# Down projection of an encoder layer: low parts of weights on VectorE alone, and quarter sums in another form

## The chip, the cores and the metric

The kernel runs on one core of a Trainium2 chip. The metric is the device time of one execution in microseconds (us), the median over several runs. Five engines work beside each other, each through its own queue in order: TensorE (PE; PEld is its weight load), VectorE (DVE), ScalarE (ACT), GpSimd (POOL), and SyncE (SP), which here only issues transfers. Engines wait for each other by semaphores.

## The reference

One encoder layer in float32 on a sequence of 1024 positions with 1024 features. The change is in its last large product:

```
x = x + g1 * (concat(y_attn, y_mem) @ w_out)
h = modulate(rms_norm(x, norm_ffn_g), sh2, sc2)
ffn = (silu(h @ w_gate) * (h @ w_up)) @ w_down      # (1024 x 2816) @ (2816 x 1024)
x = x + g2 * ffn
return rms_norm(x, final_norm_g)
```

## The kernel before

**Numbers.** Every float32 matrix is split into a high part (rounded to fp32r by a ScalarE copy, `hi`) and a low part (the rest, `lo`, a subtraction `src - hi`). A product is three matmuls: high x high, low x high and high x low (`mm3`, lines 298 to 300). In the tile names of the profile `wch` and `wcl` are the high and low part of a weight piece of the down projection, `whi` and `wlo` those of a piece of the activations; `wst` is the staging tile into which the activations come from DRAM.

**Seven products instead of eight.** The down projection is cut into 2 x 2 blocks and done by Winograd's form of Strassen's scheme, in the order of `DOWN`: 11, 21, T2, T3, T1, 22, T4. Each product runs over 11 pieces of the hidden dimension, and a piece is 4 row tiles x 3 matmuls of 128x128 by 128x512 (T4 runs twice at half width). The first five pieces of product 11 are made earlier by other code. For piece p the weights are in two tiles `wd` of 128x1024: `WD[0,p]` holds the quarters a11 and a21, `WD[1,p]` holds a12 and a22. In the rows below `wd_11122` to `wd_11126` and `wd_11105` to `wd_11110` are `WD[0,0]` to `WD[0,10]`, and `wd_11111` to `wd_11121` are `WD[1,0]` to `WD[1,10]`; `s` is a tile of 128x512 for a sum. The weights of the products are 11: a11; 21: a12; T2: a21 + a22 - a11; T3: a11 - a21; T1: a21 + a22; 22: a12 - (a21 + a22 - a11); T4: a22. Quarters that are not needed any more are overwritten by sums, in place.

**What makes a weight piece.** `load_w` (line 1487) takes the next (product, piece), and chains: the flags that must be set (`ok`), the sums (`steps`, on VectorE), `hi` on ScalarE, `lo`. The low part is made on VectorE for the products 11, 21, 22 and T4, and on GpSimd for T2, T3 and T1 (`eng`). `wch` and `wcl` have four buffers each, so a piece's high part waits until TensorE is through with the piece four before. GpSimd also makes the low parts of the activations, one per piece (`split`, line 436). At the end of a product VectorE adds the four banks in PSUM to the rows of x, once for each cell that the product belongs to (`finish`, line 1558: 16 additions for 11, 4 for 21, 12 for T2, 8 for T3, 8 for T1). After product 21 four rows are complete; ScalarE squares them (`ssb`, `sqb`) and VectorE sums the squares (`ssb<-ssb,sqb`).

**The order.** The program is recorded by a planner (`Clock`) that keeps an estimated time for each engine; `ck.chain` records each step when the planner's clock reaches it, so an edit of the steps moves the order of instructions on the engines around it. On the chip each engine follows that order, and the semaphores only delay it.

Of the kernel before, what the change touches and what calls it, by code (L numbers as in the profile page):

```python
# [11 lines left out]
F32 = mybir.dt.float32  # L12
# [8 lines left out]
P = 128  # L21
# [3 lines left out]
HALF = 512  # L25
# [215 lines left out]
def layer_kernel(ctx, tc, xT, c, w_ada, vecs, cons, rope, w_f, w_t0, w_t, w_o, w_gu, w_d, out):  # L241
# [65 lines left out]
    def halves(n):  # L307
        return slice(n * HALF, (n + 1) * HALF)

    ck = Clock()  # L310
    dve, act, gps = Engine(ck, nc.vector, "dve"), Engine(ck, nc.scalar, "act"), Engine(ck, nc.gpsimd, "gps")
# [39 lines left out]
    with tc.manual_schedule():  # L351
# [1103 lines left out]
        WE = {q: [None, None, Flag()] for q in wseq}  # L1455
        todo = []

        def open_down():
            rest = []

            def rows(c, p):
                WD[c, p] = pb.tile([P, D], F32, tag=f"wd{c}{p}", name=f"wd{c}{p}")
                rest.append((lambda: WD[c, p], w_d[2 * p + c], wd_ok[c, p]))

            for p in range(KB, NP):
                rows(0, p)
            for p in range(NP):
                rows(1, p)
            for p in range(KB):
                rows(0, p)  # L1470
            todo[0:0] = rest[0:NP - KB]
            reload("T4")
            todo.extend(rest[NP - KB:])
            opened3.set(ck, ck.t)
            load_rows()
            for _ in range(4):
                load_w()
# [9 lines left out]
        def load_w():  # L1487
            if not wseq:
                return
            q = m, c, p = wseq.pop(0)  # L1490
            e = WE[q]
            if m == "T4":
                if c == 0:
                    t = pb.tile([P, 2, HALF], F32R, tag=f"wd0{p}", name="a22")
                    e[:2] = t[:, 0], t[:, 1]
                    WE[m, 1, p] = e
                    a22 = WD[1, p][:, halves(1)]
                    ck.chain(0.0, lambda: act.activation(t[:, 0], a22, AF.Copy),
                             lambda: dve.tensor_sub(t[:, 1], a22, t[:, 0].bitcast(F32)), flag=e[2])
                return  # L1500
            a11, a12, a21, a22 = (WD[x, p][:, halves(r)] for r in range(2) for x in range(2))
            src = {"11": a11, "21": a12, "T3": a11, "T1": a21, "22": a12, "T4": a22}.get(m)
            ok = [wd_ok[x, p] for x in ((0,) if m in ("11", "T3") else (1,) if m in ("21", "22", "T4") else (0, 1))]
            steps = []
            if m == "T2":
                src = pb.tile([P, HALF], F32, tag="s", name="s", bufs=3)
                steps = [lambda: dve.tensor_add(src, a21, a22), lambda: dve.tensor_sub(src, src, a11),
                         lambda: dve.tensor_sub(a12, a12, src)]
            elif m == "T3":
                steps = [lambda: dve.tensor_sub(a11, a11, a21)]  # L1510
            elif m == "T1":
                steps = [lambda: dve.tensor_add(a21, a21, a22)]
            eng = dve if m in ("11", "21", "22", "T4") else gps

            def hi():
                e[0] = pb.tile([P, HALF], F32R, tag="wch", name="wch", bufs=4)
                act.activation(e[0], src, AF.Copy)

            def lo():
                e[1] = pb.tile([P, HALF], F32R, tag="wcl", name="wcl", bufs=4)  # L1520
                eng.tensor_sub(e[1], src, e[0].bitcast(F32))

            ck.chain(0.0, *ok, *steps, hi, lo, flag=e[2])

        def down():
            i = start["down"]
            flat = lambda t: t.rearrange("p a b -> p (a b)")
            for m in DOWN:
                for c in range(2 if m == "T4" else 1):
                    w = 256 if m == "T4" else HALF  # L1530
                    banks = []
                    for p in range(NP):
                        t = pieces[i]
                        early = m == "11" and p < KB
                        a = pieces[i + 1] if early else WE[m, c, p]
                        i += 2 if early else 1
                        yield [t[2], a[2]]
                        wt = [flat(x) for x in a[:2]] if early else a[:2]
                        for o in range(4):
                            if p == 0:  # L1540
                                yield [slot("acc")]
                                banks.append(psum_tile([P, w], "acc"))
                            mm3(banks[o][0], [x[:, o * P:(o + 1) * P] for x in wt], [flat(x) for x in t[:2]],
                                p == 0, p == NP - 1)
                            ck.pe(0.65 * w / HALF)
                        load_piece()
                        if early:
                            load_piece()
                        if opened3.done and not early:
                            load_w()  # L1550
                        if m == "22" and p < 4:
                            load_w()
                        load_rows()
                    finish(m, c, banks)
# [427 lines left out]
        pb = ctx.enter_context(tc.tile_pool(name="pb", bufs=1))  # L1982
# [80 lines left out]
```

## Time and profile before

| what | value |
|---|---|
| median of 3 runs | 1428.02 us (1427.50 to 1428.83) |
| the profiled execution | 1430.91 us, span 1429.1 us |
| mean granted TensorE clock | 0.967 |
| busy in the span: PE, DVE, ACT, POOL | 1312.8 us (92%), 1078.9 us (75%), 660.8 us (46%), 792.5 us (55%) |
| first matmul of 21, T2, T3, T1, 22, T4 | 1209.17, 1240.00, 1285.53, 1319.81, 1351.71, 1382.07 us |

Times in the rows of the trace are in us from the start of the span: start, duration, engine, line, operation, tile written, tiles read. A bracket at the end of a row tells how long the engine had been idle before it and what ended that. Nearly all of VectorE, ScalarE and GpSimd has line 96, the helper that records an instruction, so rows are told apart by tiles.

### The profile page before, as it was taken

Reading aid. Unit: us, or ns where it says so; the run is one execution under the profiler, and the core shown is the slowest. Engines: PE = TensorE matmul, PEld = TensorE weight load, DVE = VectorE, ACT = ScalarE, POOL = GpSimd, SP = SyncE. Lnnn points to the kernel's source line nnn. Section 1 sums busy time; section 2 is a strip of 40 time slices with the busy share of each in tenths; the row PEclk is TensorE's granted clock in tenths of the full one; section 3 lists DMA queues with packets and bytes.
Section 4 is the critical chain, followed back from the end, with each engine's and each line's share of the span. In section 5 each row is a group of like instructions: output and inputs, shape, how many; then the busy total and the mean of one; then the engine's idle time right before and its main releaser. Section 6 shows DMA issues by size and latency. Waiting matters only on the chain.

```text
span 1429.1 us, 19533 instructions
## 1 busy us (share of the span) xinstructions
PE 1312.8 (92%) x6602; PEld 1079.3 (76%) x6602; DVE 1078.9 (75%) x1542; ACT 660.8 (46%) x1192; POOL 792.5 (55%) x624
## 2 busy tenths in 40 slices
PE   5789799999999989999986999999999999979997
PEld 2578677888877978877764788888888887757786
DVE  6947979986887948677699786676666653999676
ACT  5444326677666655454564333333233234434462
POOL 4555554544345336677658554454454445789942
PEclk8899999999999999999999999999999999989999
DMA  7546452322121155743542333323233259622324
GB/s 280 165 123 198 136 169 78 118 65 64 52 60 58 36 162 181 255 159 122 184 155 72 105 126 103 111 97 104 103 111 111 69 188 330 238 69 87 104 63 152
DMA packets 103172, 184.40 MB, mean 129 GB/s; under 512 B 11296, under 2 KB 32672, under 8 KB 103072
## 3 DMA queue, kind: packets, MB, share of 16 engines
q1 hardware_dynamic: 89968, 161.06, 35.3%
q10 hardware_dynamic: 13104, 22.10, 4.2%
q8 instruction: 52, 0.85, 0.3%
q14 instruction: 48, 0.39, 0.1%
HBM read 136.19 MB, written 43.25 MB: 126 GB/s over the span
## 4 chain that ended last, share of the span: by engine, by line
PE 54%; DVE 21%; issue 8%; DMA 6%; POOL 5%; ACT 4%; SPq 1%; DVEq 0%; ACTq 0%; POOLq 0%
PE acc L299 13%; PE acc L300 13%; PE acc L298 13%; DVE x L96 4%; DVE ada L96 3%; POOL wlo L96 3%; DVE sst L96 3%; PE av L1028 2%; PE T L1009 2%; DVE PT L96 2%; DVE y L96 2%; PE S L977 2%; PE acct L298 2%; PE acct L300 1%; PE acct L299 1%
## 5 line engine op out<-in xcount | busy, mean ns | idle before, releaser
L96 POOL TENSOR_TENSOR wlo<-wst,whi 128x512 fp32r<-128x512 f32 (+2 forms) x208 | 304.9, 1471 | 212.1 <-ACT whi L96 190.0
L96 ACT ACTIVATE whi<-wst 128x512 fp32r<-128x512 f32 (+2 forms) x219 | 131.5, 605 | 128.2 <-DMA wst<-in_w_f_dram 22.0
L96 POOL TENSOR_SCALAR P<-P,sst 128x1024 f32<-128x1024 f32 x64 | 88.6, 1388 | 143.0 <-DVE sst L96 104.8
L299 PE MATMUL acc<-x,whi 128*128 128x512 f32 x352 | 139.9, 397 | 1.1 <-DVE x L96 1.1
L96 POOL TENSOR_TENSOR wlo<-wr,whi 128x512 fp32r<-128x512 f32 x60 | 82.9, 1382 | 80.9 <-ACT whi L96 80.9
L298 PE MATMUL acc<-hh,whi 128*128 128x512 f32 x224 | 98.0, 437 | 12.4 <-ACT hh L96 10.0
L300 PE MATMUL acc<-whi,wcl 128*128 128x512 f32 x244 | 98.2, 402 | 7.1 <-POOL wcl L96 7.0
L298 PE MATMUL acc<-whi,wch 128*128 128x512 f32 x244 | 97.1, 398 | 7.6 <-ACT wch L96 7.6
L96 ACT ACTIVATE P<-S,sst,colq 128x1024 f32<-128x1024 f32 x64 | 77.2, 1206 | 52.4 <-DVE sst L96 48.0
L299 PE MATMUL acc<-hl,whi 128*128 128x512 f32 x224 | 93.4, 417 | 8.5 <-POOL hl L96 4.8
L299 PE MATMUL acc<-wlo,wch 128*128 128x512 f32 x244 | 97.2, 398 | 0.1
L96 DVE SCALAR_TENSOR_TENSOR ada<-ada,cond 128x512 f32<-128x512 f32 (+1 forms) x79 | 79.0, 1008 | 19.6 <-DMA ada<-in_w_ada_dram 14.1
L300 PE MATMUL acc<-hh,wlo 128*128 128x512 f32 x224 | 92.5, 413 | 0.0
L96 DVE TENSOR_TENSOR sg<-acc,sg 128x512 f32<-128x512 f32 x67 | 45.4, 687 | 60.4 <-PE acc L300 60.0
L96 ACT ACTIVATE PT<-T 128x512 fp32r<-128x512 f32 x128 | 71.4, 596 | 39.8 <-PE T L1009 39.0
L96 DVE TENSOR_TENSOR PT<-T,PT 128x512 fp32r<-128x512 f32 x128 | 82.8, 682 | 7.6 <-ACT PT L96 7.5
L96 ACT ACTIVATE whi<-wr 128x512 fp32r<-128x512 f32 x60 | 37.8, 632 | 109.3 <-PE acc L299 47.3
L298 PE MATMUL acct<-whi,hh 128*128 128x256 f32 (+1 forms) x256 | 79.6, 311 | 2.3 <-DVE avt L96 0.9
L96 POOL TENSOR_TENSOR wlo<-s,whi 128x512 fp32r<-128x512 f32 x44 | 59.4, 1351 | 38.0 <-ACT whi L96 32.1
L299 PEld LDWEIGHTS acc<-x,whi 128*128 128x128 f32 x352 | 66.7, 190 | 16.7 <-DVE x L96 1.6
L1009 PE MATMUL T<-con,P 128*128 128x128 f32 x512 | 71.1, 277 | 8.8 <-DVE PT L96 6.1
L96 DVE TENSOR_REDUCE sst<-S 128x1 f32<-128x1024 f32 x64 | 77.7, 1214 | 1.8 <-PE S L977 1.6
(457 smaller groups left out, 3883.3 us busy)
## 6 DMA issues: line engine op xcount, KB each, us to landing
wr<-in_w_gu_dram SPq DMA_DIRECT2D x66, 256.0 KB, 2.8
ada<-in_w_ada_dram SPq DMA_DIRECT2D x64, 256.0 KB, 3.5
wd<-in_w_d_dram SPq DMA_DIRECT2D x22, 512.0 KB, 7.0
wst<-in_w_gu_dram SPq DMA_DIRECT2D x34, 256.0 KB, 3.1
wst<-act_d SPq DMA_DIRECT2D x33, 256.0 KB, 4.3
ada<-in_w_ada_dram SPq DMA_DIRECT2D x16, 512.0 KB, 5.5
wst<-in_w_o_dram SPq DMA_DIRECT2D x32, 256.0 KB, 3.8
act_d<-sg ACTq DMA_DIRECT2D x31, 256.0 KB, 2.1
```

The source lines that it names most:

```text
L96: return fn(*args, **kw)
L298: nc.tensor.matmul(acc, w[0], x[0], start=first, stop=False)
L299: nc.tensor.matmul(acc, w[0], x[1], start=False, stop=False)
L300: nc.tensor.matmul(acc, w[1], x[0], start=False, stop=last)
L977: nc.tensor.matmul(sp[:, halves(n)], qs[:, j * P:(j + 1) * P], k2[g][m][:, halves(n)], start=m == 0, stop=m == 1)
L1009: nc.tensor.transpose(tp[:, k], Pt[q][:, (4 * b + k) * P:(4 * b + k + 1) * P], ident)
L1028: nc.tensor.matmul(av, va[:, k, h // 4], PT[it][m][:, k], start=(k, m) == (0, 0), stop=(k, m) == (NJ - 1, 1))
```

## The change

All weight pieces get their low part from VectorE. The sums have another form. For T2 the piece first does a11 := a11 - a21 in place, which is the weight of T3, and then s := a22 - a11, which is a21 + a22 - the old a11. So T3 has no sum of its own any more and the first sum of T2 falls away: three sums of T2 and one of T3 become two and one deferred. The third, a12 := a12 - s, for product 22, is recorded after T2's low part (`rest`) instead of ahead of its high part. s has five buffers instead of three. Flags of earlier products are added to `ok`, since a11 is overwritten earlier and T3 and 22 now rely on T2's chain.

```diff
-            steps = []
+            steps, rest = [], []
             if m == "T2":
-                src = pb.tile([P, HALF], F32, tag="s", name="s", bufs=3)
-                steps = [lambda: dve.tensor_add(src, a21, a22), lambda: dve.tensor_sub(src, src, a11),
-                         lambda: dve.tensor_sub(a12, a12, src)]
-            elif m == "T3":
-                steps = [lambda: dve.tensor_sub(a11, a11, a21)]
+
+                src = pb.tile([P, HALF], F32, tag="s", name="s", bufs=5)
+                if ("11", 0, p) in WE:
+                    ok.append(WE["11", 0, p][2])
+                ok.append(WE["21", 0, p][2])
+                steps = [lambda: dve.tensor_sub(a11, a11, a21), lambda: dve.tensor_sub(src, a22, a11)]
+                rest = [lambda: dve.tensor_sub(a12, a12, src)]
+            elif m in ("T3", "22"):
+                ok.append(WE["T2", 0, p][2])
             elif m == "T1":
+                ok.append(WE["T3", 0, p][2])
                 steps = [lambda: dve.tensor_add(a21, a21, a22)]
-            eng = dve if m in ("11", "21", "22", "T4") else gps
+            eng = dve
...
-            ck.chain(0.0, *ok, *steps, hi, lo, flag=e[2])
+            ck.chain(0.0, *ok, *steps, hi, lo, *rest, flag=e[2])
```

**How the order moves.** The order of TensorE and of SyncE is the same in both programs. VectorE at the start of T2, right behind the last low part of product 21, before:

```order
L96 TENSOR_TENSOR s<-wd_11122,wd_11111 128x512
L96 TENSOR_TENSOR s<-s,wd_11122 128x512
L96 TENSOR_TENSOR wd_11111<-wd_11111,s 128x512
L96 TENSOR_TENSOR s<-wd_11123,wd_11112 128x512
L96 TENSOR_TENSOR s<-s,wd_11123 128x512
L96 TENSOR_TENSOR wd_11112<-wd_11112,s 128x512
L96 TENSOR_TENSOR s<-wd_11124,wd_11113 128x512
L96 TENSOR_TENSOR s<-s,wd_11124 128x512
L96 TENSOR_TENSOR wd_11113<-wd_11113,s 128x512
L96 TENSOR_TENSOR s<-wd_11125,wd_11114 128x512
```

and at the same place in the changed program:

```order
L96 TENSOR_TENSOR wd_11122<-wd_11122 128x512
L96 TENSOR_TENSOR s<-wd_11111,wd_11122 128x512
L96 TENSOR_TENSOR wcl<-s,wch 128x512
L96 TENSOR_TENSOR wd_11111<-wd_11111,s 128x512
L96 TENSOR_TENSOR wd_11123<-wd_11123 128x512
L96 TENSOR_TENSOR s<-wd_11112,wd_11123 128x512
L96 TENSOR_TENSOR wcl<-s,wch 128x512
L96 TENSOR_TENSOR wd_11124<-wd_11124 128x512
L96 TENSOR_TENSOR wd_11112<-wd_11112,s 128x512
L96 TENSOR_TENSOR s<-wd_11113,wd_11124 128x512
L96 TENSOR_TENSOR wd_11125<-wd_11125 128x512
L96 TENSOR_TENSOR wcl<-s,wch 128x512
```

Each piece has four rows instead of three, and its low part (`wcl<-s,wch`) stands between the sums. Behind either piece of order the four additions of product 21 follow (`x<-acc,mod,x`). Some rows later in the changed program, VectorE around the fourth and fifth piece (`s` of the fourth is made from `wd_11114` two rows ahead of these):

```order
L96 TENSOR_TENSOR wd_11126<-wd_11126 128x512
L96 TENSOR_TENSOR ssb<-ssb,sqb 128x512 x2
L96 TENSOR_TENSOR wd_11105<-wd_11105 128x512
L96 TENSOR_TENSOR s<-wd_11115,wd_11126 128x512
L96 TENSOR_TENSOR ssb<-ssb,sqb 128x512
L96 TENSOR_TENSOR wcl<-s,wch 128x512
L96 TENSOR_TENSOR s<-wd_11116,wd_11105 128x512
L96 TENSOR_TENSOR wd_11106<-wd_11106 128x512
L96 TENSOR_TENSOR wd_11114<-wd_11114,s 128x512
L96 TENSOR_TENSOR wcl<-s,wch 128x512
```

The low part of the fourth piece stands behind all three sums of squares. GpSimd in T3, before:

```order
L96 TENSOR_TENSOR wcl<-wd_11124,wch 128x512
L96 TENSOR_TENSOR wlo<-wst,whi 128x512
L96 TENSOR_TENSOR wcl<-wd_11125,wch 128x512
L96 TENSOR_TENSOR wlo<-wst,whi 128x512
L96 TENSOR_TENSOR wcl<-wd_11126,wch 128x512
```

and GpSimd in the changed program, from the last pieces of the gate and up projections through the whole down projection:

```order
L96 TENSOR_TENSOR wlo<-wr,whi 128x512 x2
L96 TENSOR_TENSOR wlo<-wst,whi 128x512 x71
L96 TENSOR_TENSOR wlo<-wst,whi 128x256 x11
L96 TENSOR_TENSOR x_10971<-x_10971,ny 128x512
```

Only the low parts of activations are left there.

## The prediction

> **What bounds the kernel now.** I began with the waits of TensorE in the last 250 us, because the change touches only the down projection. Then I cut that projection at its products (a product is 11 pieces of 12 matmuls; its first matmul is found by counting). The columns are busy us (and instructions) of PE, PEld, DVE, ACT and POOL, then clock, DMA share and GB/s; the rows are 21, T2, T3, T1 and 22.
>
> ```profile
> PE acc L298 <- ACT wch L96: 7.6, 3, 6.0
> PE acc L300 <- POOL wcl L96: 7.0, 12, 1.3
> ...
> 1209.17:1240.00 30.83, 30.83 (x134) 24.62 (x133) 29.04 (x32) 14.17 (x23) 19.64 (x13) 1.00 0.84 316
> 1240.00:1285.53 45.53, 35.04 (x133) 25.64 (x132) 45.15 (x37) 17.39 (x32) 38.37 (x24) 0.89 0.26 74
> 1285.53:1319.81 34.28, 31.97 (x134) 24.30 (x133) 31.27 (x28) 14.53 (x25) 34.28 (x24) 1.00 0.30 87
> 1319.81:1351.71 31.90, 31.13 (x133) 24.56 (x132) 18.01 (x16) 12.72 (x23) 31.90 (x24) 1.00 0.31 92
> 1351.71:1382.07 30.36, 30.36 (x134) 24.82 (x132) 21.66 (x30) 16.32 (x31) 14.55 (x12) 1.00 0.27 81
> ```
>
> Product 22 runs with TensorE never idle: 30.36 us is what a product costs when its inputs are there (132 matmuls of 0.23 us). Against that T2 loses 15.2 us, T3 3.9 and T1 1.5, together 20.6 us. That is all this change can win. In T2 DVE is full (45.15 of 45.53), in T3 and T1 POOL is (34.28 of 34.28, 31.90 of 31.90). The DMA share is a third or less, so transfers bound none of the three.
>
> How VectorE and GpSimd hinder each other is read from single rows (start, duration):
>
> ```profile
> 1251.36 0.68 DVE L96 TENSOR_TENSOR wd<-wd,s 128x512 f32<-128x512 f32 x1
> 1251.97 0.68 DVE L96 TENSOR_TENSOR ssb<-ssb,sqb 128x512 f32<-128x512 f32 x1
> 1252.57 0.68 DVE L96 TENSOR_TENSOR s<-s,wd 128x512 f32<-128x512 f32 x1
> ...
> 1255.45 1.75 DVE L96 TENSOR_TENSOR wd<-wd,s 128x512 f32<-128x512 f32 x1
> 1257.13 1.76 DVE L96 TENSOR_TENSOR s<-s,wd 128x512 f32<-128x512 f32 x1
> 1258.81 1.77 DVE L96 TENSOR_TENSOR s<-wd,wd 128x512 f32<-128x512 f32 x1
> ...
> 1272.12 1.67 DVE L96 TENSOR_TENSOR wd<-wd,s 128x512 f32<-128x512 f32 x1
> ...
> 1280.23 1.67 DVE L96 TENSOR_TENSOR wd<-wd,s 128x512 f32<-128x512 f32 x1
> ```
> ```profile
> 1265.10 1.74 POOL L96 TENSOR_TENSOR wcl<-s,wch 128x512 fp32r<-128x512 f32 x1
> 1266.80 1.74 POOL L96 TENSOR_TENSOR wlo<-wst,whi 128x512 fp32r<-128x512 f32 x1
> ...
> 1289.81 1.28 POOL L96 TENSOR_TENSOR wlo<-wst,whi 128x512 fp32r<-128x512 f32 x1
> 1291.06 1.30 POOL L96 TENSOR_TENSOR wcl<-wd,wch 128x512 fp32r<-128x512 f32 x1
> 1292.32 1.29 POOL L96 TENSOR_TENSOR wlo<-wst,whi 128x512 fp32r<-128x512 f32 x1
> ```
> ```profile
> 1245.85 2.71 DVE L96 SCALAR_TENSOR_TENSOR x<-acc,mod,x 128x512 f32<-128x512 f32 x4
> ```
> ```profile
> 1245.34 1.74 POOL L96 TENSOR_TENSOR wlo<-wst,whi 128x512 fp32r<-128x512 f32 x1
> ```
>
> While POOL is idle DVE's sums follow each other every 0.60 us. While DVE works on PSUM, POOL's instructions follow each other every 1.25. When both have sums of two SBUF operands they take turns, one of each per 1.70 us. So a POOL turn takes 1.70 - 0.60 = 1.10 from DVE. The eviction that reads PSUM takes no turn: four last 2.71, 0.67 each, with POOL at work until 1247.1. Check of the two prices: from 1255.45 to the next product's first sum at 1281.83 DVE ran 18 sums and POOL 14 instructions; 18 x 0.60 + 14 x 1.10 = 26.2, measured 26.38.
>
> The Trainium skill (SBUF — State Buffer, "Who interferes with whom") says that a VectorE instruction with two SBUF inputs and a GpSimd instruction that reads SBUF exclude each other for the whole instruction, and the loser fully blocks. By that a pair would take 0.60 + 1.25 = 1.85; the rows say 1.70, so turns are taken, with 0.15 overlapped. By the rule's 1.25 the T2 walk below would be 14 x 0.15 = 2.1 us longer and the result 1420.2; the check above speaks for 1.10.
>
> T2 has one more stall of its own, the longest of all:
>
> ```profile
> 1247.98 0.40 PE L300 MATMUL acc<-whi,wcl 128*128 128x512 f32 x1
> 1254.42 0.79 PE L298 MATMUL acc<-whi,wch 128*128 128x512 f32 x1 [6.04 <-ACT wch L96]
> 1255.01 0.63 PE L299 MATMUL acc<-wlo,wch 128*128 128x512 f32 x1
> 1256.70 0.80 PE L300 MATMUL acc<-whi,wcl 128*128 128x512 f32 x1 [1.06 <-POOL wcl L96]
> ```
> ```profile
> 1251.47 0.63 ACT L96 ACTIVATE sqb<-x 128x512 f32<-128x512 f32 x1 [1.30 <-DVE ssb L96]
> 1252.01 0.71 ACT L96 ACTIVATE x<-x,vec 128x512 f32<-128x512 f32 x1
> ...
> 1253.76 0.61 ACT L96 ACTIVATE wch<-s 128x512 fp32r<-128x512 f32 x1
> ```
>
> After three pieces (1240.0 + 3 x 2.76 = 1248.3) TensorE waits for the high part of the fourth. On ScalarE that stands behind the third square of the finished rows, which waits for a VectorE sum.
>
> **The change, part by part.** Three rows give the volume: POOL's low parts of weights, 11 and 22 of them, and the sum that goes.
>
> ```profile
> L96 POOL TENSOR_TENSOR wcl<-s,wch 128x512 fp32r<-128x512 f32 x11 | 18.9, 1719 | 2.7 <-ACT wch L96 2.7
> L96 POOL TENSOR_TENSOR wcl<-wd,wch 128x512 fp32r<-128x512 f32 x22 | 33.7, 1535 | 0.0
> L96 DVE TENSOR_TENSOR s<-s,wd 128x512 f32<-128x512 f32 x11 | 16.5, 1503 | 0.2
> ```
>
> POOL loses 33 instructions, DVE gets 33 and loses 11. Each moved low part frees 1.10 of the turns and takes 0.60. A low part on DVE is priced by the one at 1229.29 (below): 0.69 long, the next starts 0.60 later. With POOL waiting it is 1.70 at worst; I take 0.60 and count POOL's turns apart. Per piece DVE and POOL now need: T2 four sums and one turn, 3.5 us (before: (1280.23 - 1272.12)/2 = 4.05); T3 one and one, 1.70; T1 two and one, 2.30. TensorE needs 2.76. So T3 and T1 are covered and T2 is not.
>
> T2 along the new order of DVE. Its start doesn't move: the row ahead of it is the last low part of product 21, which waits for a weight buffer.
>
> ```profile
> 1229.29 0.69 DVE L96 TENSOR_TENSOR wcl<-wd,wch 128x512 fp32r<-128x512 f32 x1 [1.65 <-ACT wch L96]
> 1229.89 0.69 DVE L96 TENSOR_TENSOR s<-wd,wd 128x512 f32<-128x512 f32 x1
> ```
>
> (1) To the four evictions of product 21: 12 sums x 0.60 = 7.2, six POOL turns = 6.6 (low parts of activations, the last three of 21 and three of T2), and about 0.8 of standing, because a low part now waits in DVE's own queue for its high part (0.63 on ACT) where no other sum lies between. 1229.9 + 14.6 = 1244.5.
> (2) Four evictions, 2.7, and 0.4 until POOL lets go: 1247.6. Then seven sums (4.2), a turn, the third ssb sum and a turn (2.8): the low part of the fourth piece starts at 1254.6 and is there at 1255.3. Its high part still stands behind the third square, which waits for the first ssb sum (at 1250.0): 1250.1, two instructions of 0.54 from start to start, its own 0.63: 1251.8. So TensorE waits about 3.5 us for the high part and 2.9 for the low one; this stall is hardly shorter than before (1255.3 against 1256.7).
> (3) To the low part of the last piece: 25 sums = 15.0, six turns = 6.6, 0.75 of standing: 1277.6 to 1277.9. Ten matmuls (2.3) after that T3 begins, at 1280.3 instead of 1285.53: **5.2 us**.
>
> What is late next: the last deferred sum, two POOL turns and T3's first low part end at about 1281.3, when TensorE wants it at 1280.75. That stall of 0.6 stays of T3's 3.9: **3.3 us**. Then DVE needs 11 x 1.70 + 12 evictions x 0.67 = 26.7 in T3 and 11 x 2.30 + 8 x 0.67 = 30.7 in T1. T1 has no slack of its own (30.36), but starts from four ready buffers: **1.5 us**. In T1 a slip on DVE reaches TensorE as soon as these are used up.
>
> At nothing I cost: the waits on earlier flags (they order the recording; the data was long there), the two more s buffers (the order on SP is unchanged), and the deferred sum, which is first read by product 22, 70 us later. The new queueing is costed above: behind a low part that waits on DVE stand the next sums and the evictions; the evictions have a whole product, since four other banks are in use. Products 22 and T4 and the end keep their instructions and move forward.
>
> Sum: 5.2 + 3.3 + 1.5 = 10.0, less some 0.1 for a longer first matmul after each stall that stays: 9.9. The profiled execution (1430.91, span 1429.1) becomes 1421.0; it lay 2.9 above the median shown, so the forecast is 1428.0 - 9.9 = **1418.1**.
>
> **The rivals.**
> A, more is won: POOL, now with slack, loses turns to DVE and pushes its activations' low parts back. Four turns fewer before T2's last low part are 4.4 us: 1413.7. For it: 12 POOL instructions a product need only 15 us. Against: the turns from 1255.45 on, where DVE pushed POOL back by none.
> B, DVE stands for every high part of T2. Seven stands of 0.67 instead of 0.75 in stretch (3) are 3.9 more: 1422.0. For it: the two ends of this wait are in one queue now. Against: the order puts the next piece's sums between.
> C, slower: the same standing in all three products, at DVE's queue head. From T2's last sum at 1283.3 DVE then needs 26.7 + 11 x 0.67 for T3, and 30.7 + 11 x 0.67 for T1; with 2.3 of matmuls 22 begins at 1357.8, not 1351.7: 6.1 lost, 1434.1. It decides from 0.46 us of standing per low part (1338.3 + 29 stands = 1351.7). Against: in T3 and T1 the high parts need no fresh sum or one made a piece ahead.
> D, no change: 1428.0. Port time moved between two engines that share it wins nothing, or the end takes it back. Against the first: the sums of turns above. Against the second: in 22 TensorE never waits. The Trainium skill (Perfetto Trace Analysis, "Optimizing Scalar/DVE Operations") warns that the two share a read port, "so offloading operations between those two might not help"; by it D would be likely, but here a turn costs 1.10 on the one and 0.60 on the other.
>
> **How the numbers follow.** Chances: forecast 0.65 (its own range 1415 to 1421), A 0.12, B 0.13, C 0.05, D 0.05. A measurement of this kernel tells 0.2%, 2.9 us, from no change. Forecast, A and B are all faster: 0.90; D same: 0.05; C slower: 0.05. The range takes in A and B with a little room: 1413 to 1423.5.
>
> **What would show it.** T2 should last about 40 us, still with DVE full; T3 about 31, T1 30.4; POOL 14 to 20 us busy in each. POOL wcl must be gone from the waits of PE, and DVE wcl stand there instead, for 4 to 7 us, nearly all in T2. DVE's wcl rows should last 0.69 or 1.7, and the first stall lie at 1248 again, ending near 1255. Wrong: T2 of 44 us (B), T3 and T1 of over 33 with DVE waiting for ACT wch (C), or 22 and T4 longer (D).

## The result and the profile after

The changed kernel takes 1417.47 us (median; 1416.25 to 1419.43) beside 1427.76 us (1427.34 to 1428.83) for the kernel before on the same chip. The recorded ratio is 0.9937, 95% interval 0.9914 to 0.9959: 9.0 us faster, 5.9 to 12.3. It is not the quotient of these two medians, which lie 10.3 us apart (0.9928). The forecast was 9.9 us.

The profiled execution took 1416.67 us, with a span of 1414.9. First the stretches of its down projection. The rows are products 21, T2, T3, T1 and 22, with the same columns as in the prediction: busy us and instructions of PE, PEld, DVE, ACT and POOL, then clock, DMA share, GB/s.

```profile
1204.20:1235.02 30.82, 30.82 (x134) 24.63 (x132) 27.55 (x33) 14.00 (x23) 16.75 (x12) 1.00 0.86 317
1235.02:1276.51 41.49, 34.10 (x133) 26.38 (x132) 40.13 (x45) 18.55 (x33) 19.50 (x14) 0.88 0.27 77
1276.51:1307.73 31.22, 30.85 (x133) 24.63 (x132) 26.17 (x30) 12.70 (x22) 16.98 (x13) 1.00 0.39 109
1307.73:1338.06 30.33, 30.33 (x133) 24.79 (x132) 26.12 (x29) 12.81 (x22) 15.35 (x11) 1.00 0.36 96
1338.06:1368.42 30.36, 30.36 (x134) 24.80 (x132) 21.50 (x30) 16.31 (x31) 12.94 (x11) 1.00 0.22 67
```

T2 went from 45.53 to 41.49, T3 from 34.28 to 31.22, T1 from 31.90 to 30.33: 4.04 + 3.06 + 1.57 = 8.67 us. POOL, which filled T3 and T1, is half idle there now. T1 runs as fast as 22, so nothing holds it. What is left to win is 11 us in T2 and 0.9 in T3.

The two spans differ by 14.2 us, more than the 8.67. Of the rest, 4.97 lie ahead of product 21 (it begins at 1204.20 instead of 1209.17) and 0.55 behind the start of T4 (46.48 instead of 47.03). The 4.97 do not belong to the change: in the runs below, kernels that contain the change begin product 21 anywhere from 1202.4 to 1209.9, while their stretches repeat. So every experiment is read by its stretches, and its total only by the recorded ratio.

What TensorE waited for in the last 250 us (total us, times, longest), and the first stall of T2 row by row (start, duration, and in brackets the idle time before):

```profile
PE acc L298 <- ACT wch L96: 5.7, 3, 4.0
PE acc L300 <- DVE wcl L96: 2.8, 2, 2.4
```
```profile
1243.01 0.40 PE L300 MATMUL acc<-whi,wcl 128*128 128x512 f32 x1
1247.43 0.80 PE L298 MATMUL acc<-whi,wch 128*128 128x512 f32 x1 [4.03 <-ACT wch L96]
1248.02 0.63 PE L299 MATMUL acc<-wlo,wch 128*128 128x512 f32 x1
1251.09 0.80 PE L300 MATMUL acc<-whi,wcl 128*128 128x512 f32 x1 [2.44 <-DVE wcl L96]
1251.69 0.63 PE L298 MATMUL acc<-whi,wch 128*128 128x512 f32 x1
```

The twelve waits for POOL are gone. The stall at the fourth piece is still there, split in two: 4.03 us for the high part and 2.44 for the low part, 6.5 in place of 6.04 + 1.06.

The end of T2 is still set by VectorE. At the last piece TensorE waits once more for a high part, whose sum VectorE begins at 1271.90 (rows below). The first row is from this profile, the second from the repetition of the same kernel (the change again, below):

```profile
1273.36 0.50 PE L298 MATMUL acc<-whi,wch 128*128 128x512 f32 x1 [0.92 <-ACT wch L96]
1274.06 0.50 PE L298 MATMUL acc<-whi,wch 128*128 128x512 f32 x1 [0.35 <-ACT wch L96]
```

In the repetition the matmuls behind the first stall run late by 0.6 us more, this last wait is shorter by as much, and T2 is as long (41.48 beside 41.49). So what TensorE loses in between doesn't move the end.

The low parts of T2, two of its first rows and its last rows on VectorE:

```profile
L96 DVE TENSOR_TENSOR wcl<-s,wch 128x512 fp32r<-128x512 f32 x11 | 10.0, 906 | 2.8 <-ACT wch L96 2.8
```
```profile
1228.08 0.93 DVE L96 TENSOR_TENSOR wcl<-s,wch 128x512 fp32r<-128x512 f32 x1 [0.78 <-ACT wch L96]
...
1233.92 0.69 DVE L96 TENSOR_TENSOR wcl<-s,wch 128x512 fp32r<-128x512 f32 x1 [0.78 <-ACT wch L96]
...
1268.97 0.69 DVE L96 TENSOR_TENSOR wcl<-s,wch 128x512 fp32r<-128x512 f32 x1 [0.16 <-ACT wch L96]
...
1271.90 0.68 DVE L96 TENSOR_TENSOR s<-wd,wd 128x512 f32<-128x512 f32 x1
1273.34 0.69 DVE L96 TENSOR_TENSOR wcl<-s,wch 128x512 fp32r<-128x512 f32 x1 [0.76 <-ACT wch L96]
```

The eleven low parts of T2 made VectorE stand for 2.8 us in all. The last row shows why: where no other sum lies between `s` and its low part, VectorE stands 0.76 us for the high part (0.78 in the first two rows). Where one does, it stands 0.16 to 0.18 or not at all.

### The profile page after: what moved, and what is told of

The parts are those of the page before. It is cut to its first block, busy times and chain, and to the rows that moved or that the text cites. A ratio compares the mean times of both kernels' runs of the same rounds, so it can differ in the third digit from the quotient of the medians.

```text
span 1414.9 us, 19493 instructions
## 1 busy us (share of the span) xinstructions
PE 1305.6 (92%) x6594; PEld 1076.0 (76%) x6602; DVE 1078.5 (76%) x1564; ACT 660.8 (47%) x1192; POOL 733.9 (52%) x591
## 4 chain that ended last, share of the span: by engine, by line
PE 60%; DVE 21%; DMA 6%; issue 5%; ACT 4%; POOL 4%; SPq 1%; ACTq 0%; DVEq 0%; POOLq 0%
PE acc L299 15%; PE acc L298 15%; PE acc L300 15%; DVE x L96 4%; DVE ada L96 3%; PE av L1028 3%; DVE sst L96 2%; PE T L1009 2%; DVE PT L96 2%; PE S L977 2%; DVE y L96 1%; PE acct L298 1%; PE acct L300 1%; PE acct L299 1%; DMA qd<-q_d 1%
## 5 line engine op out<-in xcount | busy, mean ns | idle before, releaser
L96 POOL TENSOR_TENSOR wlo<-wst,whi 128x512 fp32r<-128x512 f32 (+2 forms) x208 | 297.5, 1436 | 261.2 <-ACT whi L96 249.8
L96 DVE TENSOR_TENSOR wcl<-wd,wch 128x512 fp32r<-128x512 f32 x50 | 50.9, 1031 | 38.6 <-ACT wch L96 38.3
L1009 PE MATMUL T<-con,P 128*128 128x128 f32 x512 | 70.3, 275 | 10.3 <-DVE PT L96 7.4
```

The costliest lines, as they stand in the source:

```text
L96: return fn(*args, **kw)
L1009: nc.tensor.transpose(tp[:, k], Pt[q][:, (4 * b + k) * P:(4 * b + k + 1) * P], ident)
```

## The experiments

The table gives the stretches of every run in us, and the recorded ratio of its time to that of the kernel before on the same chip (it differs from the quotient of the medians by up to 0.001). A product without waits is 30.3, so three are 91.1 (3 x 30.36).

| kernel | T2 | T3 | T1 | sum | ratio, 95% |
|---|---|---|---|---|---|
| before | 45.53 | 34.28 | 31.90 | 111.71 | 1 |
| the change | 41.49 | 31.22 | 30.33 | 103.04 | 0.9937 (0.9914 to 0.9959) |
| the change again | 41.48 | 31.20 | 30.32 | 103.00 | 0.9929 (0.9902 to 0.9955) |
| low parts alone | 44.02 | 37.14 | 30.32 | 111.48 | 0.9986 (0.9973 to 0.9998) |
| sums alone | 44.15 | 31.07 | 31.05 | 106.27 | 0.9959 (0.9943 to 0.9976) |
| third sum ahead | 43.92 | 30.31 | 30.33 | 104.56 | 0.9937 (0.9922 to 0.9952) |
| activations too | 36.95 | 30.31 | 30.33 | 97.59 | 0.9885 (0.9868 to 0.9903) |
| squares later | 38.60 | 32.78 | 31.77 | 103.15 | 0.9939 (0.9921 to 0.9957) |
| both of these | 35.26 | 30.32 | 30.32 | 95.90 | 0.9860 (0.9829 to 0.9891) |
| third sum in T1 | 40.60 | 30.31 | 30.33 | 101.24 | 0.9928 (0.9900 to 0.9956) |
| all three | 31.09 | 30.32 | 30.33 | 91.74 | 0.9844 (0.9821 to 0.9867) |

The theory is the prediction's: VectorE's own sums plus 1.10 us for each POOL turn set the end of T2, and POOL no longer sets T3 and T1. The rivals are that the order around the low parts matters more than the count, that the port time is only moved, that the first stall is what counts, and that what was won comes from elsewhere.

**The change again**, with nothing edited, beside other kernels.

> The changed kernel once more, beside the two others on the same chip. Theory: T2 41.5, T3 31.2, T1 30.3 us again within 0.3, since the order is fixed; the time at which the down projection begins moves by some us from execution to execution, as it did between the two profiles (product 21 at 1209.2 and 1204.2 us), and the whole time with it: 1416 to 1420. Rival (the earlier begin belongs to the change): product 21 begins at 1204 again and never at 1207 or later.

The stretches repeat within 0.02 us, and the time is 1418.07 us, ratio 0.9929. Product 21 begins at 1205.08. That alone would allow that the change makes the earlier part faster. But product 21 begins at 1208.21, 1209.94 and 1207.42 in three kernels below that all hold the change (squares later, both, third sum in T1), and at 1202.42 and 1202.78 in two others. So the expectation's other reading fell: the start of the down projection wanders by some 7 us between profiles. Activations too (1202.42) and squares later (1208.21) have the same order of instructions up to the first pieces of T2.

**Low parts alone.** Against the kernel before:

```diff
-                src = pb.tile([P, HALF], F32, tag="s", name="s", bufs=3)
+                src = pb.tile([P, HALF], F32, tag="s", name="s", bufs=5)
...
-            eng = dve if m in ("11", "21", "22", "T4") else gps
+            eng = dve
```

> The first half of the change alone: all low parts of weights on VectorE, the sums as they were (three in T2 ahead of the high part, one in T3), s with five buffers. Theory of turns and order: T2 still needs four VectorE sums and one GpSimd turn per piece (3.5 us), but now all three sums stand ahead of each high part, so the high and low parts come later than in the changed kernel: T2 about 44.4 us (before 45.5, changed 41.5), T3 needs two sums and a turn per piece instead of one and a turn and loses some 3 us more than in the changed kernel: about 33.5; T1 about 31.5. Together 2 to 3 us less than before, 1425 to 1426. Rival (GpSimd's low parts were the bound, taking them away is the whole gain): the same 8 to 10 us less as the change, about 1418.

T2 and T3 of this kernel, a wait of its TensorE in T3, and VectorE where T3 begins:

```profile
1238.86:1282.88 44.02, 33.03 (x134) 25.97 (x133) 42.20 (x49) 18.67 (x32) 20.96 (x13) 0.88 0.28 82
1282.88:1320.02 37.14, 33.58 (x134) 26.67 (x132) 30.70 (x38) 13.45 (x24) 15.43 (x12) 0.91 0.30 82
```
```profile
1298.31 0.79 PE L300 MATMUL acc<-whi,wcl 128*128 128x512 f32 x1 [2.73 <-DVE wcl L96]
```
```profile
1282.52 0.69 DVE L96 TENSOR_TENSOR wcl<-wd,wch 128x512 fp32r<-128x512 f32 x1 [0.76 <-ACT wch L96]
1283.12 1.80 DVE L96 TENSOR_TENSOR wd<-wd 128x512 f32<-128x512 f32 x1
1285.68 0.69 DVE L96 TENSOR_TENSOR wcl<-wd,wch 128x512 fp32r<-128x512 f32 x1 [0.76 <-ACT wch L96]
```

T3 missed its expectation, and to the other side: it became 2.9 us longer than before. With the old sums T3 still makes one sum per piece, ScalarE takes the high part of it and VectorE then the low part. Where nothing of the next piece lies between, a piece costs VectorE a contended sum (1.7), 0.76 of standing and 0.6: 1285.68 - 1282.52 = 3.16 us, where TensorE needs 2.76, and the 12 evictions of T2 come on top. TensorE waits twice, 0.83 us and the 2.73 shown. Behind the second wait matmuls start late for some 6 us (see the last section); such starts cost 3.3 us in this T3, which the expectation had not counted. Together that is the 6.8 above a product without waits. Of VectorE's standing only the two times 0.76 shown and one of 0.16 lie ahead of the longer wait. From 1304 on it stands for 0.76 to 1.54 us at each piece, and TensorE doesn't wait at all. So the standing of rival C is there, but it accounts for at most 1.7 us of the two waits; sums and evictions in one queue and the late matmuls make up the rest. The half alone moves the stretches by 0.2 us and the time by 0.14%.

**Sums alone.** Against the changed kernel:

```diff
-            eng = dve
+            eng = dve if m in ("11", "21", "22", "T4") else gps
```

> The other half alone: sums with one less and the last one deferred, the low parts of T2, T3 and T1 back on GpSimd. Theory of turns and order: T2 needs three VectorE sums and two turns per piece, 3 x 0.60 + 2 x 1.10 = 4.0 us against 4.05 before, and saves only at its first stall: about 43.8 us. T3 has no VectorE sum left, so GpSimd's two low parts run at 1.25 each, 2.5 us per piece, under TensorE's 2.76: about 31; T1 about 30.4 to 31.9, since its sum stays and both of GpSimd's instructions meet it. Together 4 to 6 us less than before, 1422 to 1424. Rival (the low parts' place is the whole gain): no change, 1428.

T2, T3 and T1:

```profile
1239.71:1283.86 44.15, 35.87 (x134) 26.74 (x132) 43.69 (x37) 19.23 (x34) 37.52 (x24) 0.88 0.27 77
1283.86:1314.93 31.07, 30.56 (x134) 24.72 (x132) 14.31 (x17) 12.87 (x22) 31.07 (x25) 1.00 0.36 102
1314.93:1345.98 31.05, 30.73 (x133) 24.64 (x132) 22.12 (x16) 12.80 (x22) 29.70 (x22) 1.00 0.29 85
```

As expected: a piece of T2 has three sums and two turns, 3 x 0.60 + 2 x 1.10 = 4.0, as long as before (4.05). T3 has no sum to contend with, and POOL, alone, gets its two low parts through in about the time TensorE needs, full for all of 31.07 us. The sums alone win 5.44 us of stretches, the low parts alone 0.23, together 8.67: 3.0 more than the two apart. The run before shows where: low parts on VectorE are paid back in T3 as long as T3 has a sum of its own in front of them, and the new form of the sums takes that sum away.

**The third sum ahead again**, in its old place between the sums and the high part:

```diff
-            ck.chain(0.0, *ok, *steps, hi, lo, *rest, flag=e[2])
+            ck.chain(0.0, *ok, *steps, *rest, hi, lo, flag=e[2])
```

> The changed kernel with the third sum of T2 (the one for product 22) put back ahead of the high part; nothing else. The counts per engine are those of the change. Theory: in T2 each high part waits for one sum more (0.60, or 1.70 with a turn), which the four buffers can't hide since VectorE is full: T2 about 44 us instead of 41.5; T3 and T1 as in the change. So 1420 to 1421. Rival (only the number of sums and turns counts, not their order): 1417.5 as the change.

T2 and T3, the waits of TensorE, and the low parts of T2 on VectorE:

```profile
1236.56:1280.48 43.92, 32.93 (x134) 25.90 (x133) 42.50 (x49) 19.22 (x33) 22.34 (x14) 0.88 0.29 85
1280.48:1310.79 30.31, 30.31 (x133) 24.78 (x132) 22.76 (x28) 12.69 (x22) 15.20 (x11) 1.00 0.33 96
```
```profile
PE acc L300 <- DVE wcl L96: 8.3, 2, 6.6
PE acc L298 <- ACT wch L96: 3.6, 2, 2.7
```
```profile
L96 DVE TENSOR_TENSOR wcl<-s,wch 128x512 fp32r<-128x512 f32 x11 | 10.4, 942 | 0.6 <-ACT wch L96 0.5
```

T2 becomes 2.43 us longer with the same instructions, and the wait for the fourth low part 6.6 instead of 2.4. So the place of the third sum, not only the count of sums, is worth those 2.4 us. It isn't standing: the eleven low parts of T2 stood for 0.6 us in all, less than in the change. TensorE waits for 1.69, 2.68 and 6.62 us up to the fourth piece and not once behind it, so here the first stall alone sets T2. T3 loses its rest of 0.9: VectorE is well ahead of TensorE when T3 begins. The sum of stretches says 1.5 us; the medians (1419.77 and 1417.47, equal ratios) cannot tell that from nothing.

**Activations too**: POOL gets no low part at all in T2, T3 and T1. In `down_w`, where a last field of 1 makes `split` take VectorE:

```diff
-                        out.append((a.rearrange("p (a b) -> p a b", a=n), n, P, c))
+                        out.append((a.rearrange("p (a b) -> p a b", a=n), n, P, 1 if m in ("T2", "T3", "T1") else c))
```

> The changed kernel, and the low parts of the activations of T2, T3 and T1 on VectorE too, so that GpSimd does nothing in these three products. Theory of turns: a GpSimd turn takes 1.10 us from VectorE, an instruction of its own 0.60; T2 needs five instructions per piece, 3.0 us instead of 3.5, about 35 to 36 us instead of 41.5, T3 and T1 30.4 each: 6 to 7 us less than the change, 1410 to 1412. Rival (the engines only share bandwidth, and a sum moved to the full engine costs its 0.60 there in addition): T2 gets 11 x 0.60 = 6.6 longer, 1424.

T2 and T3; then, for VectorE in T2, the group of the activations' low parts (count, busy us, mean ns, idle before), and three rows in order of time:

```profile
1233.27:1270.22 36.95, 33.45 (x134) 26.54 (x132) 36.77 (x62) 19.23 (x33) 0.00 (x0) 0.91 0.33 101
1270.22:1300.53 30.31, 30.31 (x133) 24.79 (x132) 23.46 (x39) 12.69 (x22) 0.00 (x0) 1.00 0.34 96
```
```profile
L96 DVE TENSOR_TENSOR wlo<-wst,whi 128x512 fp32r<-128x512 f32 x14 | 9.5, 681 | 0.2 <-ACT whi L96 0.2
```
```profile
1255.99 0.68 DVE L96 TENSOR_TENSOR wlo<-wst,whi 128x512 fp32r<-128x512 f32 x1
1256.59 0.68 DVE L96 TENSOR_TENSOR s<-wd,wd 128x512 f32<-128x512 f32 x1
1257.19 0.68 DVE L96 TENSOR_TENSOR wcl<-s,wch 128x512 fp32r<-128x512 f32 x1
```

This tests the price on which the whole prediction rests. With POOL silent the sums of VectorE follow at 0.60, its low parts last 0.68 instead of up to 1.8, and T2 falls by 4.54 us though VectorE has the low parts of 14 activations more there. T2 stays above the 35 to 36 us expected. By the prices the gain is 14 x (1.10 - 0.60) = 7.0. Why 2.5 are missing is in the trace: the stall at the fourth piece, 2.33 and 1.17 us, is the only wait of TensorE in T2. With the matmuls that start late behind it (3.1 us) it makes up the whole of what T2 lies above a product without waits, 6.6. VectorE's queue no longer sets the end, so shortening it further shows nothing. If the two engines merely shared a sum of port time, VectorE would have lost what POOL gave up. The kernel is 16.4 us faster than before (1413.02 us).

**Squares later**: the squares of the finished rows wait until the fourth piece of T3 is recorded, so that they do not stand ahead of T2's high parts on ScalarE:

```diff
-            ck.chain(0.0, flag, sq, lambda: act.activation(x, x, AF.Copy, scale=V("final_norm_g", o)))
+            ck.chain(0.0, flag, WE["T3", 0, 3][2], sq, lambda: act.activation(x, x, AF.Copy, scale=V("final_norm_g", o)))
```

> The changed kernel with the squares of the four finished rows (four ScalarE squares and copies, three VectorE sums) recorded only once T3's fourth weight piece is made, so that they no longer stand in T2 ahead of the fourth piece's high and low part. Theory (T2 is set by VectorE's count after the stall, the stall itself is mostly hidden): the first stall nearly goes, but T2 ends only by the three sums and their turn sooner, 2 to 3 us (38 to 39.5 us instead of 41.5), and the moved work costs T3 some 2 us there: 1417 in all, within 1 us of the change. Rival (the stall of 4.0 + 2.4 us sets T2): T2 about 35, 6 us less than the change, 1411.

T2, T3 and T1:

```profile
1239.01:1277.61 38.60, 34.19 (x134) 25.27 (x133) 37.51 (x42) 14.03 (x25) 20.10 (x14) 0.96 0.30 84
1277.61:1310.39 32.78, 31.35 (x134) 24.48 (x133) 29.11 (x31) 16.49 (x29) 18.73 (x13) 1.00 0.35 102
1310.39:1342.16 31.77, 30.86 (x134) 24.64 (x132) 27.47 (x29) 13.09 (x23) 15.49 (x12) 1.00 0.30 84
```

T2 wins 2.89 us and the sum of the three nothing (103.15 against 103.04). The squares' three sums on VectorE are only moved, into T3, which has little slack (+1.56). T1's +1.44 was not expected: in the trace TensorE waits there once, 0.77 us for a low part from VectorE, and no run tests the cause. So the first stall, the longest wait of all in the trace, is not by itself worth its 6.5 us.

**Both of these** edits together.

> Both together: activations' low parts of T2, T3 and T1 on VectorE and the squares later. Theory: T2 needs 3.0 us of VectorE per piece against TensorE's 2.76 and has no squares in it: 33 to 34.5 us, T3 and T1 30.4: 8 to 9 us less than the change, 1409. Rival (bandwidth shared): as for the activations alone, 1422 or more. If the activations alone win nothing and this one does, the squares are the cause.

T2:

```profile
1240.53:1275.79 35.26, 31.88 (x133) 24.34 (x132) 35.26 (x59) 14.48 (x25) 0.00 (x0) 1.00 0.37 112
```

T3 and T1 carry the moved squares without loss once POOL is silent. T2 is 0.8 us longer than the upper end expected: VectorE is full for all 35.26 us, TensorE waits only 3.4 us in it, and the clock is 1.00.

**The third sum in T1**: for the first five pieces the deferred sum is recorded behind T1's low part instead of T2's. This takes five sums out of T2's queue and leaves POOL and the squares as the change has them.

```diff
+        S2 = {}
...
-                src = pb.tile([P, HALF], F32, tag="s", name="s", bufs=5)
+                late = p < 5
+                src = pb.tile([P, HALF], F32, tag="sl" if late else "s", name="s", bufs=5 if late else 3)
+                S2[p] = src
...
-                rest = [lambda: dve.tensor_sub(a12, a12, src)]
+                rest = [] if late else [lambda: dve.tensor_sub(a12, a12, src)]
...
+                if m == "22":
+                    ok.append(WE["T1", 0, p][2])
...
+                if p < 5:
+                    rest = [lambda: dve.tensor_sub(a12, a12, S2[p])]
```

> The changed kernel, with the deferred third sum of T2's pieces 0 to 4 moved behind the low part of T1's piece (five tiles keep s until then, three take turns for pieces 5 to 10). VectorE loses five sums in T2 and gets them in T1, where it had 4 us to spare. Theory (T2 is set by VectorE's count from its start to the last low part): 5 x 0.60 = 3.0 us less, less what standing for the high part takes back: T2 38.5 to 40 us instead of 41.5, T3 and T1 as in the change; 1415 to 1416.5. Rival (the first stall and the standing set T2, the count does not): T2 41.5, no change against the changed kernel, 1418; or T1, with 5 sums more, loses what T2 wins.

T2 and T3, and the first stall in T2 with its end:

```profile
1238.25:1278.85 40.60, 33.80 (x134) 26.63 (x133) 39.52 (x42) 18.78 (x33) 21.01 (x15) 0.87 0.30 85
1278.85:1309.16 30.31, 30.31 (x133) 24.80 (x132) 25.15 (x30) 12.93 (x22) 16.66 (x12) 1.00 0.36 105
```
```profile
1250.99 0.80 PE L298 MATMUL acc<-whi,wch 128*128 128x512 f32 x1 [4.36 <-ACT wch L96]
1251.58 0.63 PE L299 MATMUL acc<-wlo,wch 128*128 128x512 f32 x1
1254.65 0.79 PE L300 MATMUL acc<-whi,wcl 128*128 128x512 f32 x1 [2.44 <-DVE wcl L96]
...
1260.20 0.39 PE L298 MATMUL acc<-whi,wch 128*128 128x512 f32 x1
```

T2 won only 0.9 us where five sums at 0.60 are 3.0, and came out above what was expected. With fewer sums VectorE no longer sets its end; the first stall does, the only wait of TensorE in T2. T2 lies 10.24 us above a product without waits, and this stall accounts for nearly all of it: 4.36 + 2.44 of waiting, and then matmuls that start late: the 13 from 1254.65 to 1260.20 take 5.55 us where 13 x 0.23 = 2.99 would do, and the two at 1250.99 some 0.5 more: 9.9. So in the changed kernel two limits lie close together, VectorE's queue (T2 of 41.5) and the first stall (40.6 with five sums fewer). The edit to the queue alone shows little for that reason.

**All three**: activations too, squares later, third sum in T1.

> Activations' low parts of T2, T3 and T1 on VectorE, squares later, and the third sum of pieces 0 to 4 in T1. Theory: VectorE's count in T2 falls to 50 instructions x 0.60 = 30 us, beside 30.36 of matmuls; T2 31 to 33 us instead of 35.3 with the first two edits alone, T3 and T1 30.3 each: 17 to 20 us less than before in the three products, 1405 to 1409 with the begin of the down projection as scattered as in the other runs. Rival (what was left in T2 with the two edits, 4.9 us, is waiting for high parts on ScalarE and not VectorE's count): T2 35, 1409.5.

T2 and T3, and what TensorE waited for:

```profile
1233.58:1264.67 31.09, 30.69 (x133) 24.64 (x132) 31.09 (x52) 14.64 (x25) 0.00 (x0) 1.00 0.42 119
1264.67:1294.99 30.32, 30.32 (x133) 24.80 (x132) 27.18 (x45) 17.01 (x30) 0.00 (x0) 1.00 0.34 96
```
```profile
PE acc L300 <- DVE wcl L96: 0.4, 1, 0.4
```

As expected, T2 falls to 31.09 and the three products to 91.74 us, 0.7 above three without waits. The kernel takes 1404.78 us (1402.69 to 1406.36), just under the range expected, ratio 0.9844 (0.9821 to 0.9867): 22.3 us faster than before, some 13 faster than the change. With this nothing of note is left to win in the three products.

## Why the prediction was right, and where it was off

The mechanism of T2 was the one forecast, and so was the order of size: 9.9 us forecast; 9.0 measured (5.9 to 12.3), 10.1 in the repetition (0.9929 of 1428.45), 8.7 by the stretches. The stretches are what the change did, so the sum of 10.0 was 1.3 too high. That the medians, 10.3 apart, come nearer to it is luck: the start of the down projection wanders by more than the difference.

**T2, 5.2 forecast, 4.04 measured.** The step that was mis-sized is the standing of VectorE for a high part: 0.8 in stretch (1) and 0.75 in stretch (3), 1.55 together. The eleven low parts of T2 stood 2.8: 1.74 in stretch (1), where three stood and the forecast had one, and 1.08 in stretch (3). The difference, 1.3, is as large as the whole miss: from product 21's last low part to the end of T2's last one the forecast had 1277.7 - 1229.9 = 47.8 us, and the trace of the changed kernel has 1273.95 - 1224.91 = 49.0 (the last low part begins at 1273.34, and the next instruction follows at 1273.95). The other terms were off by 0.5 or less and nearly cancel. The prices under it held: in the stretch behind the first stall there were the 25 sums and the six turns that the forecast counted, and what they and the standing leave over is 0.3 us of 23.0.

**The Trainium skill on the port.** It (SBUF — State Buffer, "Who interferes with whom") would have put T2 at 2.1 us above the forecast's 40.3, at 42.4, and the trace shows 41.49. That is no support for an exclusive 1.85 us pair: the contended rows of the changed kernel last 1.67 to 1.80 and the excess is in the standing.

**The first stall, 3.5 and 2.9 forecast, 4.03 and 2.44 measured.** The sum, 6.5, is right, and "hardly shorter than before" too. What the prediction did not see is that this stall would end T2 by itself as soon as VectorE's queue got shorter: the run with the third sum in T1 shows it.

**T3, 3.3 forecast, 3.06 measured; T1, 1.5 forecast, 1.57 measured.** The rest of T3's stall was put at 0.6 and is 0.86 by the stretch (31.22 - 30.36), 0.4 of it as a wait of TensorE. In the trace the deferred sum begins at 1273.95 and T3's first low part at 1275.68, both contended, as the forecast has it. What the deferred sum alone is worth there no run shows: T3 is 30.31 in the third sum ahead, without it, but also in the third sum in T1, with it. In both T2 is ended by the first stall, and VectorE is further ahead when T3 begins.

**The rivals.** A (POOL loses turns) didn't happen: POOL ran 14 instructions in T2, busy for 19.50 us. B (standing for every high part) is false for the change, which stood for 2.8 us in all. T2 of 43.92 with the third sum ahead is B's number and not its mechanism, since VectorE stood for 0.6 us there. C's standing is in the change, in T1:

```profile
1322.47 0.69 DVE L96 TENSOR_TENSOR wcl<-wd,wch 128x512 fp32r<-128x512 f32 x1 [0.76 <-ACT wch L96]
...
1325.63 0.69 DVE L96 TENSOR_TENSOR wcl<-wd,wch 128x512 fp32r<-128x512 f32 x1 [0.76 <-ACT wch L96]
```

Four low parts in a row follow each other by 3.16 us there, each behind a fresh sum and 0.76 of standing, where TensorE needs 2.76. So the reason that the prediction gave, that the high parts need no fresh sum or one made a piece ahead, does not hold in T1. TensorE still never waits in T1 (30.33): what was ready ahead of it lasted to the end, as the forecast said of T1's four buffers. That T1 came out at its 1.5 us rests on this lead, of which four such pieces use some 1.6 us (4 x 0.40, an estimate from the two pitches). D is refuted by the silent POOL, with 0.60 for each sum: 4.5 us of T2 were won by moving more work onto the engine that was already full. The Trainium skill's warning about these two engines (Perfetto Trace Analysis, "Optimizing Scalar/DVE Operations") does not hold for this shape, in the direction from GpSimd to VectorE.

**The signs named.** T3 about 31, T1 30.4 (30.33) and POOL 14 to 20 us busy (19.50, 16.98, 15.35) came as said, POOL wcl left TensorE's waits, and the stall ended at 1250.96, which is 1255.9 on the clock of before (forecast: near 1255). T2 was to be about 40 and is 41.49. Among TensorE's waits DVE wcl was to stand for 4 to 7 us and stands for 2.8; 5.7 are put down to ACT wch.

## What to carry to other kernels

Price a contended pair of engines by two numbers, the pitch of the one while the other is silent and the pitch of the pair: if the difference is more than the instruction costs on the full engine, move it onto the full engine. When the producer of an intermediate value stands in the same queue as its last reader and another engine lies between, put an instruction of the next piece between them. Otherwise the engine stands for the other's time at each piece (0.76 us here), which costs as soon as that engine sets the pace. Where two limits of a stretch lie within a few us of each other, an edit that removes one looks worthless until the other is removed too; try them together before dropping either.

## What the runs showed of the hardware that was not expected

After some waits TensorE starts matmuls every 0.43 us instead of 0.23 for a while, with 0.63 instead of 0.39 for one. In the changed kernel that lasts from 1251.09 to 1256, and the granted clock of T2 is 0.88. TensorE loses about 2.4 us by it there (12 starts in 5.16 us), though T2's end, which VectorE sets, didn't move with it. It isn't only the longest waits that bring it: it followed a wait of 2.73 us in T3 of the low parts alone (0.91), of 2.33 and 1.17 with two matmuls between (activations too, 0.91), and of 1.64 and 0.41 with two between (squares later, 0.96). It didn't follow a single wait of 1.78 us (both edits, 1.00), and in T2 of the low parts alone the first matmul behind a wait of 2.68 us took 0.50. The Trainium skill (TensorE: Matmul & The Clock Gate, "Part 1: The HAM clock gate") gives an idle window of about 3.4 us for this; here shorter gaps were enough, and by what rule the runs don't show.

The start of the down projection varied from 1202.4 to 1209.9 us between profiles, and by 5.8 us between two kernels with the same instructions in the same order ahead of it (activations too, squares later), while T1 repeated within 0.02 us wherever nothing held it. A difference of two spans alone would have put the gain of this change at 14.2 us.
